# S5 branch: the lag blocks' B comes by DMA, their rows lie as (group, channel), and ScalarE places the old states

## The chip, the core and the metric

One core of a Trainium2 chip runs the kernel: TensorE (matmuls), VectorE, ScalarE and GpSimd (elementwise work), and SyncE (SP), whose queue issues every DMA of this kernel. The metric is the device time of one execution in microseconds, as the median of several runs.

## What is computed

One step of a decoder layer for a prompt of 512 tokens and 8 samples of 4 tokens (544 tokens in all, 1024 channels). The normed input is projected once; four branches (SSD, S5, mLSTM, attention into a memory) work on their columns; each is projected down, the four are merged by gates, projected out and added to the input. The change lies in the S5 branch alone:

```
lam_bar = exp(lam * dt);  b_bar = ((lam_bar - 1) / lam)[..., None] * complex(b_re, b_im)
bu = einsum('gnc,btgc->btgn', b_bar, u)          # 64 groups of 16 channels, 64 complex states each
bu[:, 0] += lam_bar * h0
h  = associative_scan(h_t = lam_bar * h_(t-1) + bu_t)
y  = einsum('gcn,btgn->btgc', c, h).real + d_skip * u
```

## The kernel before

All large products go through `unit` (line 166): a weight block of 1024x128 comes by DMA (`load`, line 80, `raw`, three buffers), is split into a high part (`whi`, ScalarE, line 177) and a low part (`wlo`, VectorE, line 64 by way of line 178), and 24 x 2 matmuls (line 188) give one `pu` of 128x544. The instructions of an engine run in the order of its queue; that order is laid down when the kernel is built, by a planner that may move an instruction ahead of others as soon as its inputs and its buffer are free in its own estimate. So the order on a queue is not always the order of the lines. Waits between engines and for buffers are put in by the same layer.

The S5 branch works in 8 rounds `f` of 128 channels, that is 8 groups of 16 channels. Time is cut into blocks of 8 steps, and a round has four parts:

- `s5_in(f)` (line 697): the input columns `pu`, copied into `uf`, turned by way of DRAM (`ud`) into `U`, with (step in block, channel) on the rows.
- `s5_mats(f)` (line 714): the matrices of the round. `bm` and `cm` are powers of lam_bar times B and C, made by VectorE and GpSimd together with temporaries `q1`, `q2`. `bbs` (line 749) is B alone, with the real parts on rows 0 to 63 and the imaginary parts on rows 64 to 127: four copies by VectorE from `bbr` and `bbi` (line 752), which `s5_setup` has made once. Eight small matmuls (line 756) of `bbs` and `cm` give `pk`, the response of one channel to another at lags 0 to 7 within a block. `pk` is copied in four pieces, by VectorE and ScalarE in turn, into `kt` (line 761), 16 rows (channel in group) by 8 groups; GpSimd makes `dk`, the skip term `d` on a diagonal, and adds it at lag 0 (lines 763, 764). `kt` goes to DRAM (`kd`, line 767) behind a stretch of zeros, and is read back (`tp`, line 769) shifted by row, so that it becomes a triangular block matrix.
- `s5_scan(f)` (line 772): `bt` times `U` gives `pv`; after a rotation by `E` (a table in `stag`, "st" in the rows, made by GpSimd in `s5_rot`, line 640, for two rounds at a time, behind rounds 0, 2 and 4) the recurrence is a real scan (lines 795, 796); rotated back it is stored in `hs` (lines 811, 812), whose first 8 columns are the samples' old states `h0`, placed by four VectorE copies (line 814). The last VectorE operations make the samples' new states `hn` from `pv` (lines 821 to 823).
- `s5_y(f)` (line 826): `tp` times `U` plus `cm` times `hs` gives `py` (lines 834, 835), copied to `yj` by ScalarE (line 836) and turned by way of DRAM (`yd`, `yt`) for `s5_out` (line 843), which applies `permid` and the GELU.

`s5_mats(f + 1)` is written behind `s5_scan(f)`. Between these parts steps of `gate_down` (line 211, `gd`) put in units of the gates and of the down projection of the attention branch: TensorE's large work in this stage. There are four PSUM banks for everything small (`bank`, line 48): `pv` takes two of them until `hn` is made, `pk`, `pbt`, `pn` and `py` take the others in turn. `bbs` and `dk` share one buffer (tag `bbs`), `hs` has one buffer, `tp` has two.

## Time and profile before

| | us |
|---|---|
| median of 3 runs | 1527.41 |
| lowest and highest | 1520.2, 1528.18 |
| the profiled execution | 1523.98 |
| its span, first to last instruction | 1522.2 |
| TensorE busy | 1446.7 |
| VectorE busy | 925.6 |
| ScalarE busy | 485.5 |
| GpSimd busy | 349.2 |

The profile names the engines PE (TensorE's matmuls), PEld (its weight loads), DVE (VectorE), ACT (ScalarE), POOL (GpSimd) and SPq (SyncE's DMA issues). All times within it are microseconds from the span's start unless marked ns. A row of instructions gives the engine, the line of the kernel (that of a helper where a helper issues it), what is written from what, and the shapes. Line 64 is every `tensor_tensor`, line 61 every copy by way of `copy`, line 67 every `scalar_tensor_tensor`. A wait is put down to the event that came last before the engine went on.

### The profile page before, as it was taken

What the parts mean: (1) busy time and instruction counts of PE and PEld (TensorE: products, weight loads), DVE (VectorE), ACT (ScalarE), POOL (GpSimd) and SP (SyncE); (2) the same over time, 40 slices, a digit from 0 to 9 for tenths busy, and PEclk for the clock granted to TensorE, in tenths of its full rate; (3) what the DMA queues carried; (4) which work ended last, traced back from release to release, by engine and by line L of the source; (5) the groups of instructions that cost most, each with busy time, mean ns of one, the idle gap of its engine ahead of it and who ended that gap; (6) DMA issues with size and microseconds to landing.
All of it is one profiled execution on the core that took longest, in us unless ns stands there. A gap on an engine that the chain in (4) does not pass through costs nothing.

```text
span 1522.2 us, 28087 instructions
## 1 busy us (share of the span) xinstructions
PE 1446.7 (95%) x11505; PEld 1364.3 (90%) x11505; DVE 925.6 (61%) x1810; ACT 485.5 (32%) x825; POOL 349.2 (23%) x527
## 2 busy tenths in 40 slices
PE   6999999789879899999999999999999999899997
PEld 6988888678768899999999989999999998789997
DVE  6355487898778768486787644354343456554543
ACT  5244333222222333243333322243332332113332
POOL 2000133766465201101232322100000011110222
PEclk9999999999789999999999999999999999999999
DMA  8577362435334333322222355222222225673341
GB/s 200 159 215 221 99 200 59 106 93 126 82 92 108 84 100 82 86 78 81 74 73 74 97 167 146 70 70 77 77 78 74 79 82 176 197 218 113 94 146 59
DMA packets 288034, 171.75 MB, mean 113 GB/s; under 512 B 36934, under 2 KB 278922, under 8 KB 287907
## 3 DMA queue, kind: packets, MB, share of 16 engines
q1 hardware_dynamic: 287906, 169.97, 40.4%
q8 instruction: 90, 1.47, 0.4%
q14 instruction: 38, 0.30, 0.1%
HBM read 145.35 MB, written 24.60 MB: 112 GB/s over the span
## 4 chain that ended last, share of the span: by engine, by line
PE 63%; DVE 10%; DMA 4%; issue 3%; POOL 2%; ACT 1%; SPq 0%; POOLq 0%; ACTq 0%; DVEq 0%
PE pu L188 48%; PE pu L1644 3%; DVE wlo L64 2%; DVE hs L64 1%; DMA raw<-in_w_out_dram 1%; DMA yd<-yj 1%; PE pacc L1557 1%; DVE bbs L752 1%; DVE cm L67 1%; PE pcu L1442 1%; DMA out_dram<-cb 1%; PE pn L1436 1%; PE py L834 1%; PE py L835 1%; DMA cb<-in_state_mlstm_c_dram 1%
## 5 line engine op out<-in xcount | busy, mean ns | idle before, releaser
L188 PE MATMUL pu<-xh,whi 128*128 128x272 f32 (+1 forms) x2000 | 432.8, 294 | 1.3 <-DVE uf L706 1.1
L188 PE MATMUL pu<-xh,wlo 128*128 128x272 f32 (+1 forms) x2000 | 428.9, 293 | 0.0
L188 PE MATMUL pu<-xl,whi 128*128 128x272 f32 (+1 forms) x2000 | 428.2, 292 | 0.6 <-DVE xl L64 0.6
L64 DVE TENSOR_TENSOR wlo<-raw,whi 128x1024 fp32r<-128x1024 f32 x181 | 251.5, 1390 | 226.3 <-ACT whi L177 221.1
L177 ACT CAST whi<-raw 128x1024 fp32r<-128x1024 f32 x181 | 198.9, 1099 | 502.6 <-PE pu L188 373.1
L188 PEld LDWEIGHTS pu<-xh,whi 128*128 128x128 f32 x2000 | 322.1, 191 | 8.3 <-issue 6.2
L188 PEld LDWEIGHTS pu<-xl,whi 128*128 128x128 f32 x2000 | 322.2, 192 | 5.6 <-issue 4.5
L188 PEld LDWEIGHTS pu<-xh,wlo 128*128 128x128 f32 x2000 | 320.2, 191 | 5.5 <-issue 5.1
L188 PE MATMUL pu<-oh,wlo 128*128 128x272 f32 x640 | 135.6, 292 | 6.0 <-DVE wlo L64 6.0
L188 PE MATMUL pu<-oh,whi 128*128 128x272 f32 x640 | 136.5, 292 | 0.0
L188 PE MATMUL pu<-ol,whi 128*128 128x272 f32 x640 | 136.4, 292 | 0.0
L188 PEld LDWEIGHTS pu<-oh,wlo 128*128 128x128 f32 x640 | 102.0, 191 | 7.7 <-DVE wlo L64 6.6
L188 PEld LDWEIGHTS pu<-ol,whi 128*128 128x128 f32 x640 | 102.7, 191 | 1.6 <-issue 1.5
L188 PEld LDWEIGHTS pu<-oh,whi 128*128 128x128 f32 x640 | 102.9, 191 | 1.0 <-issue 0.8
L64 POOL TENSOR_TENSOR merged<-merged,gt 128x544 f32<-128x544 f32 x18 | 29.1, 1616 | 142.0 <-DVE gt L67 141.9
L67 DVE SCALAR_TENSOR_TENSOR cb<-cb,dcm,pcn 128x257 f32<-128x257 f32 x64 | 28.5, 478 | 26.4 <-PE pcn L1563 26.1
L834 PE MATMUL py<-U,tp 128*128 128x72 f32 x128 | 28.3, 307 | 13.8 <-DVE hn L64 7.1
L67 DVE SCALAR_TENSOR_TENSOR cc<-cc,dcm,pcu 128x257 f32<-128x257 f32 x24 | 11.5, 478 | 44.4 <-PE pcu L1442 44.4
L188 PE MATMUL pu<-mh,whi 128*128 128x256 f32 x128 | 37.7, 294 | 0.1
L188 PE MATMUL pu<-mlo,whi 128*128 128x256 f32 x128 | 37.7, 295 | 0.0
L64 POOL TENSOR_TENSOR SS<-SS,dec 128x128 f32<-128x128 f32 x24 | 19.5, 814 | 77.6 <-DVE SS L1210 49.8
L188 PE MATMUL pu<-mh,wlo 128*128 128x256 f32 x128 | 36.2, 283 | 0.0
(641 smaller groups left out, 2297.7 us busy)
## 6 DMA issues: line engine op xcount, KB each, us to landing
raw<-in_w_in_dram SPq DMA_DIRECT2D x124, 512.0 KB
raw<-in_w_down_dram SPq DMA_DIRECT2D x32, 512.0 KB
kb<-in_cache_mem_k_dram SPq DMA_DIRECT2D x8, 1024.0 KB
raw<-in_w_mem_kv_dram SPq DMA_DIRECT2D x16, 512.0 KB
vb<-in_cache_mem_v_dram SPq DMA_DIRECT2D x16, 512.0 KB
cb<-in_state_mlstm_c_dram SPq DMA_DIRECT2D x16, 512.0 KB
out_dram<-cb SPq DMA_DIRECT2D x16, 512.0 KB
tp<-kd SPq DMA_DIRECT2D x8, 512.0 KB
```

Of the source, the lines that this page charges most:

```text
L64: eng.tensor_tensor(out, a, b, op)
L67: V.scalar_tensor_tensor(out, a, s, b, op0, op1)
L177: S.copy(hv, rv)
L188: T.matmul(ps[:, a, 0:c1 - c0], wt[:, k, :], xt[:, k, c0:c1], start=first, stop=last)
L752: V.tensor_copy(bbs[64 * ri:64 * ri + 64, :, g2, :], src[64 * g2:64 * g2 + 64, gs])
L834: T.matmul(o, tp[:, g, :], U[:, g, 0:72], start=True, stop=False)
L835: T.matmul(o, cm[:, g, 1:9, :].rearrange("p l c -> p (l c)"), hs_[:, g, 0:72], start=False, stop=True)
L1436: T.matmul(p2[:, 0:257], qh[:, dt, sl], cc[:, dt, 0:257], start=dt == 0, stop=dt == 1)
L1442: T.matmul(p3[:, 0:CE], k_[:, dt * P:(dt + 1) * P], v_, start=j == 0, stop=j == 2)
L1557: T.matmul(pacc[32 * h:32 * h + 32, 0:257], qm[:, 2 * h + dt, :], cbs_[h // 2][:, 2 * (h % 2) + dt, 0:257], start=b == 0 and dt == 0, stop ...
L1644: T.matmul(pu, wt[:, k, :], mk[:, t0:t1], start=k == 0 and j == 0, stop=k == NK - 1 and j == 2)
```

## The change

Three things, all in the S5 branch. The four VectorE copies that fill `bbs` become four DMAs from the same sources, and `bbs` gets two buffers of its own. The lag matmuls take all 32 columns of `bbs` of a pair of groups at once, so that `pk` and `kt` lie on 128 rows (4 pairs x 2 groups x 16 channels) by 2 x 128 columns; of the 2 x 2 combinations of groups only the two equal ones are used. `kt` is one ScalarE copy; the skip term is one VectorE operation on lag 0, from a column `dcol` and a constant `i16` that are made once; `dk` and GpSimd's two operations go. `kd` is written by four DMAs of 32 rows, the zeros in front of it by eight in place of two, and `tp` becomes two tiles, each read by a DMA of half the size. The old states are placed in `hs` by ScalarE, not by VectorE.

```diff
--- before.py
+++ after.py
@@ -401,11 +401,11 @@
     crs = [mtemp(512).rearrange("p (b g n) -> p b g n", b=4, g=2) for _ in range(2)]
     hrs = mtemp(512).rearrange("p (r q n) -> p r q n", r=2, q=2)
     s5b1 = mtemp(512)
-    s5b2 = mtemp(320)
+    s5b2 = mtemp(192)
     s5tmp = mtemp(384).rearrange("p (i a) -> p i a", a=32)
     ldv = mtemp(4)[0:32]
-    sdg = mtemp(16)[0:64]
-    s5_loads = [(sdg, I["s5_d"][0].rearrange("(g c) -> g c", c=16)), (ldv[:, 0:2], I["s5_log_dt"][0].rearrange("(a b) -> a b", b=2))]
+    sdg = mtemp(128)[0:8]
+    s5_loads = [(sdg, I["s5_d"][0].rearrange("(f p) -> f p", p=P)), (ldv[:, 0:2], I["s5_log_dt"][0].rearrange("(a b) -> a b", b=2))]
     for i, nm in enumerate(("re", "im")):
         s5_loads.append((arow[:, i, :], I["s5_a_" + nm][0].rearrange("(a b) n -> a (b n)", b=2)))
         s5_loads.append((bri[:, i], I["s5_b_" + nm][0].rearrange("(a b) n c -> (b n) a c", b=2)))
@@ -522,7 +522,8 @@
     h0 = pt_([P, 2, NB, 32], "h0")
     hn = pt_([P, 2, NB, 32], "hn")
     hp = pt_([P, 64], "hp")
-    d16 = pt_([16, 64], "d16")
+    dcol = pt_([P, 8], "dcol")
+    i16 = pt_([P, 16], "i16")
 
     def s5_setup():
         dtv = ldv[:, 2:4]
@@ -631,8 +632,9 @@
 
         yield
         pd = bank("pd")
-        T.transpose(pd[0:16, 0:64], sdg, ident[0:64, 0:64])
-        V.tensor_copy(d16, pd[0:16, 0:64])
+        T.transpose(pd[:, 0:8], sdg, ident[0:8, 0:8])
+        V.tensor_copy(dcol, pd[:, 0:8])
+        V.tensor_reduce(i16, ident.rearrange("p (b c) -> p c b", c=16), AX.X, ADD)
 
     hd = heads_()
     pacc = pst.tile([P, 512], F32, name="pacc4", tag="bk")
@@ -688,11 +690,12 @@
     s5d = s5c.enter_context(tc.tile_pool(name="s5d", bufs=2, space=bass.MemoryType.DRAM))
     s5r = s5c.enter_context(tc.tile_pool(name="s5r", bufs=1, side="right", reuse_waits="tile"))
 
-    kds = [s5d.tile([16, 8, 240], F32, name=f"kd{i}", tag=f"kd{i}", bufs=1) for i in range(2)]
-    kz = s5r.tile([16, 8, P], F32, name="kz", tag="kt")
+    kds = [s5d.tile([32, 4, 2, 240], F32, name=f"kd{i}", tag=f"kd{i}", bufs=1) for i in range(2)]
+    kz = s5r.tile([P, 2, P], F32, name="kz", tag="kt")
     G.memset(kz, 0.0)
     for kd in kds:
-        dma(kd[:, :, 0:112], kz[:, :, 0:112])
+        for a in range(4):
+            dma(kd[:, a, :, 0:112], kz[32 * a:32 * a + 32, :, 0:112])
 
     def s5_in(f):
         pu = unit(wcols(C_U + f * P), x2, perm=True)
@@ -746,27 +749,28 @@
             pr = slice(64 * g2, 64 * g2 + 64)
             stt(cmv[64:128, :, g2], q1[pr], -1.0, q2[pr], MUL, SUB)
 
-        bbs = s5r.tile([P, 4, 2, 16], F32, name="bbs", tag="bbs")
+        bbs = s5r.tile([P, 4, 2, 16], F32, name="bbs", tag="bbs", bufs=2)
         for ri, src in enumerate((bbr, bbi)):
             for g2 in range(2):
-                V.tensor_copy(bbs[64 * ri:64 * ri + 64, :, g2, :], src[64 * g2:64 * g2 + 64, gs])
+                dma(bbs[64 * ri:64 * ri + 64, :, g2, :], src[64 * g2:64 * g2 + 64, gs])
+
         pk = bank("pk")
         for g2 in range(2):
             for a in range(4):
-                T.matmul(pk[32 * a:32 * a + 16, g2 * P:(g2 + 1) * P], bbs[:, a, g2, :],
+                T.matmul(pk[32 * a:32 * a + 32, g2 * P:(g2 + 1) * P], bbs[:, a].rearrange("p g c -> p (g c)"),
                          cm[:, 2 * a + g2, 0:8, :].rearrange("p l c -> p (l c)"), start=True, stop=True,
                          tile_position=(0, 32 * a))
-        kt = s5r.tile([16, 8, P], F32, name="kt", tag="kt")
+        kt = s5r.tile([P, 2, P], F32, name="kt", tag="kt")
+        S.copy(kt.rearrange("p g x -> p (g x)"), pk[:, 0:256])
+        stt(kt[:, :, 0:16], bc(i16, 1, 2), dcol[:, f:f + 1], kt[:, :, 0:16], MUL, ADD)
+
+        kd = kds[f % 2]
         for a in range(4):
-            copy(S if a % 2 else V, kt[:, 2 * a:2 * a + 2, :].rearrange("p g x -> p (g x)"), pk[32 * a:32 * a + 16, 0:256])
-        dk = s5r.tile([16, 8, 16], F32, name="dk", tag="bbs")
-        tt(G, dk, bc(ident[0:16, 0:16], 1, 8), bc(d16[:, 8 * f:8 * f + 8], 2, 16), MUL)
-        tt(G, kt[:, :, 0:16], kt[:, :, 0:16], dk, ADD)
-
-        kd = kds[f % 2]
-        dma(kd[:, :, 112:240], kt)
-        tp = s5r.tile([P, 8, P], F32, name="tp", tag="tp", bufs=2)
-        dma(tp, bass.AP(tensor=kd.tensor, offset=kd.offset, ap=[[16, 8], [8 * 240, 16], [240, 8], [1, P]]))
+            dma(kd[:, a, :, 112:240], kt[32 * a:32 * a + 32])
+        tp = [s5r.tile([P, 4, P], F32, name="tp", tag=f"tp{g2}", bufs=2) for g2 in range(2)]
+        for g2 in range(2):
+            dma(tp[g2], bass.AP(tensor=kd.tensor, offset=kd.offset + g2 * (16 * 1920 + 240),
+                                         ap=[[16, 8], [1920, 16], [480, 4], [1, P]]))
         return bt, cm, tp, ev_[f // 2][:, :, f % 2]
 
     def s5_scan(f, U, bt, E):
@@ -811,7 +815,7 @@
             tt(V, hsv[0:64, :, g2, 9:73], t1[pr], t2[pr], SUB)
             tt(V, hsv[64:128, :, g2, 9:73], t3[pr], t4[pr], ADD)
             for ri in range(2):
-                V.tensor_copy(hsv[64 * ri:64 * ri + 64, :, g2, 0:8], h0[pr, ri, :, gs].rearrange("p b a -> p a b"))
+                S.copy(hsv[64 * ri:64 * ri + 64, :, g2, 0:8], h0[pr, ri, :, gs].rearrange("p b a -> p a b"))
         V.tensor_copy(hp[:, 8 * f:8 * f + 8], hs_[:, :, 72])
 
         p4 = (bc(pwr[:, 4, gs], 1, NB), bc(pwi[:, 4, gs], 1, NB))
@@ -831,7 +835,7 @@
             for g4 in range(4):
                 g = 4 * hb + g4
                 o = py[:, g4 * 72:(g4 + 1) * 72]
-                T.matmul(o, tp[:, g, :], U[:, g, 0:72], start=True, stop=False)
+                T.matmul(o, tp[g % 2][:, g // 2, :], U[:, g, 0:72], start=True, stop=False)
                 T.matmul(o, cm[:, g, 1:9, :].rearrange("p l c -> p (l c)"), hs_[:, g, 0:72], start=False, stop=True)
             S.copy(yj[:, 4 * hb:4 * hb + 4, :].rearrange("p g k -> p (g k)"), py[:, 0:288])
         yt = s5r.tile([P, 8, 72], F32, name="yt", tag="yt")
```

## Rows read from the trace of the kernel before

**Rows 1.** the page's busy line: us, share of the span, instructions of each engine

```profile
PE 1446.7 (95%) x11505; PEld 1364.3 (90%) x11505; DVE 925.6 (61%) x1810; ACT 485.5 (32%) x825; POOL 349.2 (23%) x527
```

**Rows 2.** stretches A:B: length, busy us (instructions) of each engine, clock, DMA, GB/s

```profile
250.00:530.00 280.00, 237.82 (x1918) 218.45 (x1919) 233.97 (x460) 74.36 (x127) 149.22 (x221) 0.91 0.40 95
530.00:1522.00 992.00, 975.71 (x7794) 942.49 (x7792) 547.78 (x1025) 314.77 (x521) 151.83 (x197) 0.99 0.36 103
```

**Rows 3.** TensorE's waits from 250 to 532: us in total, times, longest us

```profile
PE pk L756 <- DVE cm L67: 9.6, 7, 3.4
PE py L834 <- DVE hn L64: 7.1, 1, 7.1
PE py L834 <- DMA tp<-kd: 4.4, 1, 4.4
```

**Rows 4.** VectorE's groups by shape from 245 to 535: busy us, mean ns, idle before

```profile
L752 DVE COPY bbs<-bbr 64x64 f32<-64x64 f32 x16 | 19.5, 1218 | 0.8 <-POOL kt L64 0.5
L61 DVE COPY kt<-pk 16x256 f32<-16x256 f32 x16 | 6.6, 410 | 0.4
L814 DVE COPY hs<-h 64x32 f32<-64x32 f32 x32 | 7.9, 247 | 9.4 <-PE py L835 9.0
L64 DVE TENSOR_TENSOR hn<-hn,pvi 128x32 f32<-128x32 f32 x8 | 1.4, 180 | 0.0
```

**Rows 5.** VectorE's timeline, pairs of bbs copies: start us, us, instruction, idle before

```profile
307.92 5.41 DVE L752 COPY bbs<-bbr 64x64 f32<-64x64 f32 x2
343.91 0.39 DVE L752 COPY bbs<-bbr 64x64 f32<-64x64 f32 x2 [0.54 <-POOL kt L64]
369.75 5.20 DVE L752 COPY bbs<-bbr 64x64 f32<-64x64 f32 x2
```

**Rows 6.** the timeline around the third long pair, three engines

```profile
437.76 7.04 DVE L752 COPY bbs<-bbr 64x64 f32<-64x64 f32 x2
443.35 1.39 POOL L64 TENSOR_TENSOR st<-st,rt 128x256 f32<-128x256 f32 x2
447.58 0.70 PE L834 MATMUL py<-U,tp 128*128 128x72 f32 x2 [7.13 <-DVE hn L64]
```

**Rows 7.** TensorE's timeline after the second long pair

```profile
381.06 1.09 PE L728 MATMUL pbt<-ident,bm 128*128 128x128 f32 x8 [1.53 <-DVE bm L64]
390.62 0.63 PE L756 MATMUL pk<-cm,bbs 128*16 128x128 f32 x8 [3.39 <-DVE cm L67]
```

**Rows 8.** ScalarE from 245 to 535: a group, then two of its waits

```profile
L59 ACT COPY kt<-pk 16x256 f32<-16x256 f32 x16 | 5.8, 365 | 60.7 <-DVE kt L61 48.0 <-POOL st L64 7.4 <-issue 3.8
ACT whi L177 <- PE pu L188: 29.0, 13, 6.2
ACT yj L836 <- PE py L835: 15.8, 10, 3.1
```

**Rows 9.** SP's timeline, two issues of one round, and one of SP's waits

```profile
437.02 0.58 SPq L767 DMA_DIRECT2D kd<-kt  x1
439.38 0.63 SPq L769 DMA_DIRECT2D tp<-kd  x1
SPq L710 <- DMA ud<-uf: 32.9, 8, 4.8
```

**Rows 10.** VectorE and GpSimd during trains of GpSimd, and the group of hs

```profile
364.72 1.23 DVE L64 TENSOR_TENSOR wlo<-raw,whi 128x1024 fp32r<-128x1024 f32 x1
364.32 1.77 POOL L64 TENSOR_TENSOR st<-st,pw 128x64 f32<-128x64 f32 x2
302.64 2.62 DVE L64 TENSOR_TENSOR hs<-t,t 64x256 f32<-64x256 f32 x2
L64 DVE TENSOR_TENSOR hs<-t,t 64x256 f32<-64x256 f32 x32 | 19.6, 611 | 1.2 <-POOL t L64 0.5
```

**Rows 11.** SP's waits from 250 to 532

```profile
SPq L82 <- DVE wlo L64: 50.2, 8, 13.5
SPq L82 <- DVE s L64: 22.3, 2, 17.2
```

## The prediction

> **What bounds the kernel now.** I read the page's busy line first, then a table by stage, then who TensorE waited for in the one stage that the change touches, then the timeline around the longest of those waits. The busy line [rows 1] says TensorE: 95% of the span. A gain in work of other engines counts only where TensorE stands. The table by stage [rows 2] shows where that is: from 250 to 530 us, the S5 stage, TensorE is busy for 237.82 of 280 us, so it stands for 42.2 us, and its mean granted clock is 0.91, against 0.99 in the 992 us behind it. There VectorE is busy for 233.97 of 280 us (84%), against 55% behind (547.78 of 992). The waits of TensorE in this stage [rows 3] name VectorE nearly throughout: 9.6 us in 7 waits of the pk matmuls for cm, 7.1 us in one wait of py for hn. One wait is for a transfer (4.4 us, for tp). So inside the stage the limit is VectorE's queue, which is served in order, together with the chain of small steps that runs through it; outside the stage nothing of the change matters.
>
> **The long copies.** Of VectorE's groups in the stage [rows 4] one is out of line: 16 copies bbs<-bbr of 64x64 take 19.5 us, 1218 ns each, while a pair of the same copies takes 0.39 us where GpSimd is quiet [rows 5]. Three pairs make the difference: 5.41, 5.20 and 7.04 us. The last of them starts at 437.76 and ends at 444.80; GpSimd runs its rotation table (st, rt) without a gap until 443.35 + 1.39 = 444.74 [rows 6]. The copy waits until GpSimd's train is over. Behind it in VectorE's queue stands hn, which frees a PSUM bank, and TensorE stood 7.13 us for that before 447.58 [rows 6]. The other two have no such hole directly behind them. After the second, TensorE waited 1.53 us for bm and 3.39 us for cm [rows 7].
>
> **The change part by part.** The base is the profiled execution: 1523.98 us, of which the span is 1522.2; the median of the three times shown is 3.4 us above it, the lowest 3.8 us below.
>
> (a) bbs copies become DMAs. The three pairs are 5.41 + 5.20 + 7.04 - 3 x 0.39 = 16.5 us longer than undisturbed. What of this comes back to TensorE: the 7.1 us hole whole, of the 1.53 + 3.39 = 4.9 us half, since other work of VectorE stands in front of bm and cm too, and about 0.5 us around the first pair: 10 us. Bounds: 0, if the next VectorE instruction meets the same train of GpSimd, and 16.5. A gain above the holes is possible, since the stage's granted clock is 0.91 and may rise with fewer holes; I leave that in the range.
>
> (b) Undisturbed work leaves VectorE: 32 bbs copies at 0.19 us (half of the quiet pair), 32 hs copies at about 0.19 (a little under their mean of 0.247, which has stalls in it), 16 kt copies at 0.41 [rows 4]; 8 new scalar_tensor_tensor of 128x32 come in, which I price as the nearest 128x32 addition, 0.18 us [rows 4]. 6.1 + 6.1 + 6.6 - 1.4 = 17.4 us less in 280. It returns only where VectorE is the late one. I take a quarter, 4 us; bounds 0 and 17.4.
>
> (c) The hs copies move to ScalarE. In the stage VectorE stood 9.0 us before them, for the py matmuls to release hs [rows 4]; behind it stood the cm operations of the next group, on which pk waits. On ScalarE, the two yj copies wait for the same matmuls anyway (15.8 us in 10 waits [rows 8]), so a copy queued behind yj waits for nothing new. Work of ScalarE: 32 copies of 64x32, each between VectorE's 0.19 us and the 0.365 us of ScalarE's 16x256 copy [rows 8]; I take 0.25, so 8 us, less 8 kt copies at 0.365: 5 us more on an engine that is busy 74 of 280 us [rows 2]. I take a gain of 2 us; bounds -9 (the whole wait now stands in front of a whi cast and from there of TensorE) and +9.
>
> (d) One kt copy instead of four. Now VectorE and ScalarE alternate, and ScalarE waited 48.0 us for VectorE in that [rows 8]; two GpSimd operations, dk and the addition to kt, end the chain. Afterwards ScalarE copies once (128x256, which I price as its 16x256, 0.365 us), and VectorE adds the skip term. That shortens the way from pk to kd and frees the pk bank sooner, but TensorE waited for tp only once, 4.4 us [rows 3], so I count no gain. The added wait is VectorE's, for ScalarE's copy: behind it VectorE's whole queue stands. Bounds: nothing, if ScalarE is ready, to 6.2 us a group, the longest time that ScalarE's whi cast waited in the stage [rows 8]. I take nothing, because ScalarE idles for three quarters of the stage.
>
> (e) More transfers on SP's queue: per group four for bbs, three more for kd, one more for tp. At 0.58 to 0.63 us an issue [rows 9] that is 8 x 0.6 = 4.8 us of issuing per group, in 280 / 8 = 35 us; SP has the room. Kd takes 2.36 us from its issue to that of tp [rows 9]; with four issues in a row the last lands 3 x 0.58 = 1.7 us later, which (d)'s shorter chain should pay. Six more zero fills at the same price are 3.5 us once, at the start of the stage. A bbs transfer has 256 runs of only 64 bytes, and no row shows one alone: its bounds are kd's 2.36 us (128 runs) and the 4.8 us that SP stood at longest for ud, with 1024 runs [rows 9]; I take 2.4, nearest in count. It reads only bbr and bbi, which the setup has made before the first group, and with two buffers it can run a group ahead. I take -1 us, with 0 and -3.5 as bounds; how it could be much more is a rival.
>
> Sum: 10 + 4 + 2 + 0 - 1 = 15 us. 1523.98 - 15 = 1509 for an execution like the profiled one; with the 3.4 us to the median, **1512**.
>
> **A rule against the change.** In the quiet stretches the copies cost 0.39 us a pair, and in a train of GpSimd the whole train: that is what the rows show. The Trainium skill, page "SBUF — State Buffer", section "Who interferes with whom", says that a VectorE instruction with two SBUF inputs also contends with a GpSimd instruction that reads SBUF, and that the loser is blocked fully. By that rule, taking the copies out would only hand the stall to wlo or hs, which have two such inputs. The trace is divided: wlo at 364.72 took 1.23 us in the middle of a train, and it was GpSimd's pair beside it that stretched to 1.77 us; but a pair hs<-t,t took 2.62 us at 302.64, where the 64x256 operations of that name average 0.61 [rows 10]. By the rule the time would be the first rival's 1522, by the wlo row the forecast's 1512.
>
> **Rivals.** First, **the stall moves**: the operations that follow in VectorE's queue read two SBUF tiles, and meet the same trains. Then (a) gives nothing: 4 + 2 - 1 = 5 us, 1522. For it: hs at 302.64; against it: wlo at 364.72, which got its turn inside a train where the copies waited for the end [rows 6, 10]. Chance 0.2.
>
> Second, slower: **bbs lands too late**. SP's queue is in order, and it often stands: 50.2 us in 8 waits of the weight loads for wlo, and one of its waits for s was 17.2 us [rows 11]. In the kernel before, bbs was ready about 15 us ahead of pk (the long pair of 369.75 ends at 374.95, the next pair takes 0.4, pk runs at 390.62 [rows 5, 7]). If the four transfers are queued behind a stall like the longest, pk comes 17.2 + 4 x 0.58 + 2.4 - 15 = 6.9 us late, and the TensorE work queued behind it too. It turns the change into a loss from the third such group on (20.7 against 15). With four of the eight groups hit: 4 x 6.9 - 15 = 12.6 us lost, 1540. Against it: the second buffer and inputs that are ready early. Chance 0.12.
>
> Third, **ScalarE becomes the place to wait**: its in-order queue holds hs until py is done, and VectorE waits for kt. The 9.0 us of (c) then turn from +2 to -9: 15 - 11 = 4 us gained, 1523. Chance 0.13. Last, the order in which the instructions stand in the queues shifts, and the holes stay where they were in size: no change, 1527, chance 0.05.
>
> **How the numbers follow.** The forecast has 0.5. Its own range goes from 1497 (all of (a), half of (b), half of the 9.0 in (c): 16.5 + 8.7 + 4.5 = 30 us) to about 1519. To hold 8 in 10 the range must take in the first and third rival and the near end of the second: 1496 to 1532. The far end of the second and that of (d), 6.2 us in every group, are what I leave out. About 0.5%, 7.6 us, is what a measurement of this kernel can tell from no change. Faster by more: 0.47 of the forecast and 0.1 of the near rivals, 0.57; within: 0.30; slower: 0.13, nearly all the second rival.
>
> **What would show it.** Right: no VectorE instruction of 5 us or more in the S5 stage; TensorE's 7 us wait for hn gone; VectorE's busy time in the stage down by 25 to 35 us from 234; TensorE's idle time there down from 42 us to about 30. First rival: wlo, hs or s show up with 3 to 6 us during GpSimd's trains. Second: pk waits for a transfer of bbs. Third: waits of ScalarE for py grow, and whi is late. I am wrong if the stage is no shorter though VectorE's work has fallen: then the chain of handoffs, not the queue of VectorE, sets its pace.

## The result: a gain of 27 us, nearly twice the forecast

| | before | after |
|---|---|---|
| median, us (4 runs each) | 1525.0 | 1497.63 |
| lowest and highest | 1520.2, 1528.18 | 1491.55, 1502.62 |
| the profiled execution, its span | 1523.98, 1522.2 | 1494.56, 1492.7 |

The medians differ by 27.4 us. The ratio, taken over all runs of both kernels and therefore not exactly the quotient of the medians, is 0.9825, with an interval from 0.9804 to 0.9846: 26.7 us. The time lies inside the range, at its lower end; the forecast had 15 us. The page's busy line and the two stretches of the kernel after answer to [rows 1, 2] (a stretch: length, busy us and instructions of PE, PEld, DVE, ACT, POOL, granted clock, DMA share, GB/s). The stage ends with the last py, at 530.2 before and at 503.3 after.

```profile
PE 1438.0 (96%) x11505; PEld 1359.7 (91%) x11505; DVE 889.5 (60%) x1739; ACT 490.3 (33%) x849; POOL 340.3 (23%) x511
250.00:503.30 253.30, 232.73 (x1910) 216.18 (x1909) 196.13 (x387) 78.53 (x152) 142.34 (x205) 0.93 0.46 110
503.30:1492.00 988.70, 972.56 (x7801) 939.70 (x7800) 549.16 (x1027) 315.49 (x522) 150.50 (x197) 1.00 0.36 103
```

The stage is 26.7 us shorter. TensorE's idle time in it falls from 42.2 to 253.30 - 232.73 = 20.6 us. The other 5.1 us are TensorE's own: 237.82 us busy at a mean granted clock of 0.91 before, 232.73 at 0.93 after; busy time times clock is 216.4 us in both. The 3 us by which the rest of the span is shorter lie in unchanged work at 1.00 against 0.99. VectorE's work in the stage falls by 37.8 us.

TensorE's waits from 240 to 520 us of the kernel after (us, times, longest), to hold against [rows 3]:

```profile
PE pn L850 <- DVE bt L61: 5.6, 4, 2.3
PE py L839 <- DVE hs L64: 3.7, 1, 3.7
PE pk L760 <- issue: 3.4, 1, 3.4
PE py L838 <- DVE st L67: 3.4, 3, 1.6
PE pk L760 <- DVE cm L67: 2.1, 2, 1.8
PE py L838 <- DVE hn L64: 0.7, 1, 0.7
```

The wait for hn is down from 7.1 to 0.7 us, that for cm from 9.6 to 2.1, and none for a DMA of bbs or tp is left. The waits on which the sum rested have gone. The experiments ask which part of the change took them away.

### The profile page after: what moved, and what is told of

Read it like the earlier page. It is cut to its first block, busy times and chain, and to the rows that moved or that the text cites. A ratio compares the mean times of both kernels' runs of the same rounds, so it can differ in the third digit from the quotient of the medians.

```text
span 1492.7 us, 28127 instructions
## 1 busy us (share of the span) xinstructions
PE 1438.0 (96%) x11505; PEld 1359.7 (91%) x11505; DVE 889.5 (60%) x1739; ACT 490.3 (33%) x849; POOL 340.3 (23%) x511
## 4 chain that ended last, share of the span: by engine, by line
PE 63%; DVE 7%; DMA 5%; POOL 3%; issue 2%; ACT 1%; SPq 0%; POOLq 0%; ACTq 0%; DVEq 0%
PE pu L188 48%; PE pu L1648 3%; DMA out_dram<-cb 2%; DVE wlo L64 2%; DMA raw<-in_w_out_dram 1%; PE py L839 1%; POOL st L64 1%; PE py L838 1%; POOL q L64 1%; PE pcu L1446 1%; PE pn L1440 1%; POOL rt L64 1%; PE pst L1212 1%; PE pyi L1206 1%; PE pacc L1561 1%
```

## The experiments

The ratios below are against the kernel before as it ran beside each experiment (medians of 1522 to 1523.4 us), each with its interval; the kernel after is the one of the result above. A difference between two experiments carries both intervals. "Before" and "after" name the kernel that an edit starts from. The table reads each kernel's trace from 250 us to its last py. A trace is of one execution, which need not be the median one: it lies above the median by 7 us in k2, 6 in f1, 4 in e1 and e3, and below it by 3 in the kernel after. Idle is TensorE's, busy VectorE's. "pk held" adds up over the 8 rounds the time from the last pk matmul to the end of the last copy out of pk. "pk for cm" is the total of TensorE's wait of pk for VectorE's cm. The last column has VectorE's single instructions of over 4 us.

| kernel | median | ratio | idle | busy | pk held | pk for cm | over 4 us |
|---|---|---|---|---|---|---|---|
| before | | 1 | 42.2 | 234.0 | 72 | 9.6 | bbs 5.2, 5.0, 6.7 |
| e1_dma_only | 1517.84 | 0.9959 | 44.7 | 226.5 | 64 | 4.1 | wlo 6.0, s 6.7 |
| e2_hs_act_only | 1519.55 | 0.9977 | 39.8 | 225.4 | 71 | 12.4 | bbs 5.2, 4.5, hs 7.3 |
| e4_bbs_act | 1520.72 | 0.9979 | 41.8 | 224.3 | 68 | 11.1 | s 7.3, wlo 4.6, s 6.7 |
| m1_dma_and_hs | 1520.3 | 0.9989 | 39.3 | 217.0 | 64 | 2.4 | s 5.3, hs 7.3 |
| f1_dk_own_buffer | 1526.85 | 1.003 | 41.6 | 228.4 | 71 | 8.3 | hn 5.9 |
| g1_kt_scalar | 1524.94 | 1.0019 | 39.6 | 227.4 | 13 | 3.3 | bbs 4.8, 7.5, hs 6.4 |
| f2_skip_on_dve | 1514.06 | 0.9943 | 37.2 | 223.8 | 66 | 15.5 | none |
| l1_kt_scalar_skip_dve | 1509.49 | 0.991 | 32.3 | 218.1 | 13 | 16.3 | none |
| e3_rows_only | 1505.55 | 0.9875 | 30.8 | 213.1 | 3 | 19.0 | none |
| after | 1497.63 | 0.9825 | 20.6 | 196.1 | 3 | 2.1 | none |
| e5_after_onebuf | 1495.42 | 0.9826 | 20.3 | 196.1 | 3 | 2.0 | none |
| e6_after_bbs_dve | 1497.36 | 0.9851 | 26.1 | 205.7 | 3 | 10.0 | none |
| e7_after_hs_dve | 1496.76 | 0.9822 | 21.5 | 203.1 | 3 | 2.1 | none |
| f3_after_skip_gpsimd | 1495.93 | 0.9826 | 22.2 | 192.4 | 4 | 5.8 | none |
| k2_after_four_pieces | 1501.94 | 0.9869 | 28.9 | 201.1 | 64 | 1.8 | none |

### The three parts, one at a time

**The DMA alone** (e1; before; one buffer, shared with dk as before):

```diff
-                V.tensor_copy(bbs[64 * ri:64 * ri + 64, :, g2, :], src[64 * g2:64 * g2 + 64, gs])
+                dma(bbs[64 * ri:64 * ri + 64, :, g2, :], src[64 * g2:64 * g2 + 64, gs])
```

> The kernel before with one edit: the four bbs copies are DMAs (bbs keeps its one buffer, which it shares with dk). VectorE loses 23.6 us of bbs copies, 17.5 of them stalls. Train theory (what was paid is the long pairs behind GpSimd's trains): 15 to 20 us faster. Queue theory (every us off VectorE's queue returns at the rate of the whole change, 27 us for 38, so 0.7): 23.6 x 0.7 = 17 us faster. Chain theory (the gain comes from the shorter way from pk to kd and from the work taken off GpSimd): 0 to 5 us faster. If a bbs transfer with one buffer lands too late: slower, and pk waits for a DMA.

Measured: 1517.84 us, 0.9959 [0.9934, 0.9984], 5.5 us by the medians against the 10 of step (a). Around the place of [rows 6], the timeline of this kernel (start us, us, engine, line, instruction, idle before):

```profile
436.93 6.84 DVE L64 TENSOR_TENSOR s<-pwi,h 128x32 f32<-128x32 f32 x2
442.34 1.39 POOL L64 TENSOR_TENSOR st<-st,rt 128x256 f32<-128x256 f32 x2
445.62 0.70 PE L834 MATMUL py<-U,tp 128*128 128x72 f32 x2 [6.59 <-DVE hn L64]
```

The copies are gone and the hole is still there, 6.59 us in place of 7.13. The pair that now stands at the head of VectorE's queue reads two tiles in SBUF, s<-pwi,h; it ends at 443.77, with GpSimd's train (442.34 + 1.39 = 443.73). The group's median is 0.182 us, and one of this pair took 6.743 us. That is the first rival, at that place to the letter.

A second wait is new in this kernel. From 250 to 532 us TensorE has

```profile
PE pk L756 <- DVE hs L64: 7.1, 1, 7.1
```

which the profile puts down to hs, since an hs operation ended just then. But pk does not read hs. It reads bbs, and the trace's semaphores show the two bbs<-bbi transfers of that round, issued at 291.13 and 292.22, landing at 298.66 and 298.91; pk begins at 298.91. In m1 below the profile names the transfer for the wait at the same place. In the kernel before, this pk waited 1.7 us for VectorE's bbs. This speaks for the second rival's event here too: the DMA alone gave back part of its gain in this round. Where the time goes is seen in SP's order: in e1 and m1 the bbs<-bbi transfers of the later seven rounds are issued right behind the 512 KB read of tp and land 5.1 to 8.0 us after their issue, while the bbs<-bbr transfers ahead of tp take 1.9 to 3.0 us.

**The old states on ScalarE alone** (e2; before):

```diff
-                V.tensor_copy(hsv[64 * ri:64 * ri + 64, :, g2, 0:8], h0[pr, ri, :, gs].rearrange("p b a -> p a b"))
+                S.copy(hsv[64 * ri:64 * ri + 64, :, g2, 0:8], h0[pr, ri, :, gs].rearrange("p b a -> p a b"))
```

> The kernel before with one edit: the 32 old-state copies into hs are on ScalarE. VectorE loses 7.9 us of work, and 9.0 us of waits for py stand on ScalarE. Train theory: within 2 us of before. Queue theory: 0.7 x 7.9 = 5.5 us faster, up to 12 if the waits count too. Chain theory: no change.

Measured: 1519.55, 0.9977 [0.996, 0.9994], about 3.7 us. Two of the three long pairs of bbs stay, and in place of the third another pair meets GpSimd's train:

```profile
433.89 7.76 DVE L64 TENSOR_TENSOR hs<-t,t 64x256 f32<-64x256 f32 x2
```

**The new rows alone** (e3; after, with these three lines put back: one buffer, both kinds of copies on VectorE):

```diff
-        bbs = s5r.tile([P, 4, 2, 16], F32, name="bbs", tag="bbs", bufs=2)
+        bbs = s5r.tile([P, 4, 2, 16], F32, name="bbs", tag="bbs")
-                dma(bbs[...], src[...])
+                V.tensor_copy(bbs[...], src[...])
-                S.copy(hsv[..., 0:8], h0[...])
+                V.tensor_copy(hsv[..., 0:8], h0[...])
```

> The kernel before with the new rows alone: pk and kt on 128 rows, one ScalarE copy, skip term by one VectorE operation, GpSimd's dk and kt additions gone; bbs copies and old states stay on VectorE. VectorE loses 6.6 - 2.8 = 3.8 us, GpSimd 10.5 us. Train theory: 0 to 3 us faster, and three long bbs pairs stay. Queue theory: 0.7 x 3.8 = 3 us faster. Chain theory: 10 us or more faster.

Measured: 1505.55, 0.9875 [0.9851, 0.99], 17.7 us: two thirds of the gain from the part that step (d) had priced at nothing. First its bbs copies, then its main wait of TensorE:

```profile
L755 DVE COPY bbs<-bbr 64x64 f32<-64x64 f32 x16 | 4.6, 290 | 0.1
PE pk L760 <- DVE cm L67: 19.0, 6, 7.2
```

VectorE still makes the copies here, and they take 290 ns where [rows 4] has 1218: the long pairs are gone without a copy being moved. The largest wait left is pk for cm.

**Both without the rows** (m1; before, with the edits of the first two together):

> The kernel before with the bbs DMAs and ScalarE's old states together, without the new rows: the one combination of the three parts that is missing. Alone they gave 5.5 and 3.7 us; on top of the rows either gives 8 to 9 us and both together no more. If they add without the rows: 9 us faster than before. If without the rows pk's bank and GpSimd's late table hide them: 3 to 6 us faster, no more than the DMA alone.

Measured: 1520.3, 0.9989 [0.9973, 1.0006], no difference, where the two alone gave 5.5 and 3.7 us. VectorE has 17 us less to do in the stage, and TensorE is idle for 39.3 us. Two of VectorE's pairs, then one of TensorE's waits:

```profile
305.96 5.35 DVE L64 TENSOR_TENSOR s<-pwi,h 128x32 f32<-128x32 f32 x2
434.33 7.77 DVE L64 TENSOR_TENSOR hs<-t,t 64x256 f32<-64x256 f32 x2
PE pk L756 <- DMA bbs<-bbi: 6.6, 1, 6.6
```

The stall is handed on to s and hs, and pk waits 6.6 us once for bbs: the second rival's event, in a kernel where the buffer of bbs is shared with dk. The stage ends at 530.7 us, before it ended at 530.2. By the prediction's own sign ("I am wrong if the stage is no shorter though VectorE's work has fallen"), it is the chain of handoffs that sets the pace there, and not VectorE's queue.

**ScalarE in place of the DMA** (e4; before):

```diff
-                V.tensor_copy(bbs[...], src[...])
+                S.copy(bbs[...], src[...])
```

> The kernel before with one edit: the four bbs copies are on ScalarE in place of VectorE. This takes the same work off VectorE as the DMAs do, without a transfer. Train and queue theory: as fast as the DMA alone, 15 to 20 us faster, less at most 8 us for 8 us of new work on ScalarE. Chain theory: 0 to 5 us faster. If it equals the DMA version, the DMA is only one of two ways off VectorE's queue.

Measured: 1520.72, 0.9979 [0.9963, 0.9995]. It matters little who takes the copies: the three long stalls are there again, now in s, wlo and s. One of them:

```profile
303.06 7.45 DVE L64 TENSOR_TENSOR s<-pwi,h 128x32 f32<-128x32 f32 x2
```

### The parts undone in the kernel after

**bbs by VectorE** (e6; after; two buffers kept):

```diff
-                dma(bbs[...], src[...])
+                V.tensor_copy(bbs[...], src[...])
```

> The changed kernel with the DMA undone: VectorE copies bbs again, into two buffers of its own. If the parts add up as they did one by one (5.5 for the DMA, 3.7 for the old states, 17.7 for the rows, 27 together): 5.5 us slower than the changed kernel, about 1503. Queue theory: 6.1 us of undisturbed copies come back, 0.7 x 6.1 = 4 us slower. If the DMA only removes a collision that the rows have removed already: no slower than 2 us.

Measured: 1497.36, 0.9851 [0.9813, 0.9889]: not separable from the kernel after. Its copies, VectorE's:

```profile
L755 DVE COPY bbs<-bbr 64x64 f32<-64x64 f32 x16 | 3.6, 227 | 0.1
```

**The old states by VectorE** (e7; after):

```diff
-                S.copy(hsv[..., 0:8], h0[...])
+                V.tensor_copy(hsv[..., 0:8], h0[...])
```

> The changed kernel with the old states undone: VectorE places them again. With the new rows alone the kernel was 17.7 us faster than before, with rows and old states but VectorE's bbs copies 26 us, so the old states should be worth some 8 us on top of the rows, more than the 3.7 us alone: about 1506. If the parts only add: 3.7 us slower, about 1501. If the second bbs buffer made that difference and not the old states: no slower than 2 us.

Measured: 1496.76, 0.9822 [0.98, 0.9845]. With the rows in place the hs copies can be undone for nothing, but not both parts (e3: 8 us more). Undoing the bbs DMA (e6) costs nothing by the medians and 4 us by the ratios; its interval overlaps that of the kernel after and that of e3, so it is not settled. What the two parts have in common is relief of VectorE ahead of cm: pk's wait for cm is 19.0 us with neither, 10.0 with hs moved, 2.1 with bbs moved and 2.1 with both.

**One buffer for bbs** (e5; after):

```diff
-        bbs = s5r.tile([P, 4, 2, 16], F32, name="bbs", tag="bbs", bufs=2)
+        bbs = s5r.tile([P, 4, 2, 16], F32, name="bbs", tag="bbs")
```

> The changed kernel with one bbs buffer in place of two. The rows alone had one buffer and were 17.7 us faster than before; with the old states and two buffers 26 us, though the old states can be undone for nothing. If the second buffer makes that difference: about 8 us slower than the changed kernel, 1505. If bbs is early enough in one buffer: within 3 us.

Measured: 1495.42, 0.9826 [0.9794, 0.9859]. The second buffer is worth nothing; pk does not wait for bbs here either. In both kernels bbs has landed at least 5.8 us ahead of pk in every round.

### What in the new rows does it

Three differences in the rows are tried here: pk leaves its bank in one copy, GpSimd is out of the chain from pk to kd, and dk no longer shares a buffer with bbs. A fourth, kd in four DMAs and tp in two tiles, was not tried by itself.

**dk with a buffer of its own** (f1; before; two setup columns moved to make room):

```diff
-        dk = s5r.tile([16, 8, 16], F32, name="dk", tag="bbs")
+        dk = s5r.tile([16, 8, 16], F32, name="dk", tag="dk")
```

> The kernel before with one edit: dk has a buffer of its own, so that the bbs copies of the next group need not wait for GpSimd's addition to kt (room is made by two setup tables in scratch). New rows alone gave 17.7 us, and their trace has no long bbs pair though the copies stay on VectorE. Buffer theory (the long pairs come from the shared buffer, which puts the copies into GpSimd's train): 10 us or more faster, no bbs pair over 2 us. Queue-position theory (another operation with two SBUF inputs meets the train in their place, as s did for 6.7 us when the DMA alone was put in): 0 to 4 us faster. GpSimd theory (what counts is that GpSimd's train need no longer stand behind the kt pieces): 0 to 4 us faster.

Measured: 1526.85, 1.003 [1.0016, 1.0044], slightly slower. By itself the shared buffer was not it. But the buffer theory's event came: the long bbs pairs are gone, and one long instruction is left, of hn.

```profile
L751 DVE COPY bbs<-bbr 64x64 f32<-64x64 f32 x16 | 4.3, 271 | 0.1
```

So VectorE can lose most of its long stalls without the kernel being faster. GpSimd stands 19.3 us for ScalarE's pieces in this kernel.

**The skip term on VectorE** (f2; before; GpSimd out of the chain, the four pieces stay):

```diff
-        tt(G, dk, bc(ident[0:16, 0:16], 1, 8), bc(d16[:, 8 * f:8 * f + 8], 2, 16), MUL)
-        tt(G, kt[:, :, 0:16], kt[:, :, 0:16], dk, ADD)
+        tt(V, dk, bc(ident[0:16, 0:16], 1, 8), bc(d16[:, 8 * f:8 * f + 8], 2, 16), MUL)
+        tt(V, kt[:, :, 0:16], kt[:, :, 0:16], dk, ADD)
```

> The kernel before with one edit: dk and the addition to kt are VectorE's, no longer GpSimd's; rows, the four kt pieces and the shared buffer stay. VectorE gains 16 small operations (about 4 us), GpSimd loses 10.5 us and, above all, no longer stands in its queue until the kt pieces are done. GpSimd theory: 10 us or more faster. Buffer theory and queue theory: within 4 us, rather slower, since VectorE has more to do.

Measured: 1514.06, 0.9943 [0.9923, 0.9963]. VectorE gets 16 operations more, and the kernel is faster by 9 us; no instruction of over 4 us is left. What GpSimd loses is two operations and a place where it stood. GpSimd's waits ahead of its addition to kt in the kernel before, 250 to 532 us:

```profile
POOL kt L64 <- issue: 7.7, 2, 5.3
POOL kt L64 <- DVE hp L815: 6.1, 1, 6.1
POOL kt L64 <- ACT kt L59: 2.9, 1, 2.9
```

That is 16.7 us in which the work queued behind, its rotation table among it, does not move (for 7.7 of them the profile names no event that ended the wait). Whether this standing is what costs, g1 tells. The trains are still there: GpSimd's longest stretch of work without a gap of over 0.1 us in the stage is 17.6 us here, 20.2 before and 20.2 in the kernel after.

**All four pieces on ScalarE** (g1; before; pk's bank freed at once, GpSimd stays):

```diff
-            copy(S if a % 2 else V, kt[:, 2 * a:2 * a + 2, :].rearrange("p g x -> p (g x)"), pk[32 * a:32 * a + 16, 0:256])
+            copy(S, kt[:, 2 * a:2 * a + 2, :].rearrange("p g x -> p (g x)"), pk[32 * a:32 * a + 16, 0:256])
```

> The kernel before with one edit: all four kt pieces are ScalarE's, so that they no longer alternate with VectorE; rows, dk, GpSimd's addition and the shared buffer stay. GpSimd stood in its queue for those pieces 16.7 us in the stage of before, and where it did, its rotation table ran late, into VectorE's work. Late-table theory (what is paid is that GpSimd's table runs late because GpSimd waits for the kt pieces): GpSimd's waits before kt fall to a few us, no VectorE instruction over 4 us, 8 to 15 us faster. Work theory (what counts is VectorE's 6.6 us of kt copies): 4 us faster with the waits as they are. If the four pieces are as late on ScalarE's queue: no change.

Measured: 1524.94, 1.0019 [1.0006, 1.0033], 3 us slower, though the bank does come free. The kernel before, one round: pk, the first pn, TensorE's one wait before the next pn, then three of the last events (the last ScalarE piece, GpSimd's addition, the next pn).

```profile
391.73 0.63 PE L756 MATMUL pk<-cm,bbs 128*16 128x128 f32 x8
392.46 1.32 PE L846 MATMUL pn<-yt,permid 128*128 128x272 f32 x2
405.19 0.52 PE L188 MATMUL pu<-oh,wlo 128*128 128x272 f32 x2 [2.13 <-DVE wlo L64]
405.83 0.37 ACT L59 COPY kt<-pk 16x256 f32<-16x256 f32 x1 [3.81 <-DVE kt L61]
406.33 0.45 POOL L64 TENSOR_TENSOR kt<-kt,dk 16x128 f32<-16x128 f32 x1 [6.06 <-DVE hp L815]
406.42 1.09 PE L847 MATMUL pn<-yt,permid 128*128 128x240 f32 x2
```

The same round with all pieces on ScalarE, and VectorE's longest pair:

```profile
397.41 1.49 ACT L59 COPY kt<-pk 16x256 f32<-16x256 f32 x4 [4.25 <-PE pk L756]
399.21 1.14 PE L846 MATMUL pn<-yt,permid 128*128 128x272 f32 x2
401.83 1.02 PE L847 MATMUL pn<-yt,permid 128*128 128x240 f32 x2
365.34 7.72 DVE L752 COPY bbs<-bbr 64x64 f32<-64x64 f32 x2
```

In the kernel before the second pn (406.42) starts 0.2 us behind the last piece (405.83 + 0.37), which ends 13.8 us after pk (391.73 + 0.63). TensorE did not stand idle for that: between the two pn it works on units but for the 2.13 us wait for wlo, and its waits for the last piece add up to 0.4 us in the whole stage. If the held bank cost time in this kernel, it was through the place that pn got in the queue, which no row prices. With all pieces on ScalarE, VectorE stands in GpSimd's trains for 4.8, 7.5 and 6.4 us.

This run also answers f2's question. GpSimd's addition to kt, before and here:

```profile
L64 POOL TENSOR_TENSOR kt<-kt,dk 16x128 f32<-16x128 f32 x8 | 4.0, 500 | 16.7 <-issue 7.7 <-DVE hp L815 6.1 <-ACT kt L59 2.9
L64 POOL TENSOR_TENSOR kt<-kt,dk 16x128 f32<-16x128 f32 x8 | 4.7, 593 | 0.6 <-POOL dk L64 0.5
```

GpSimd no longer stands for the pieces (0.6 us), pk's bank is free, and still the long instructions stay and nothing is gained: the late-table theory falls in this form. What g1 keeps is GpSimd's two operations and the buffer that dk shares with bbs.

**Both** (l1; before, with the edits of f2 and g1 together):

> The kernel before with two edits that were tried one by one: all four kt pieces on ScalarE (alone: 3 us slower) and the skip term on VectorE (alone: 9.4 us faster). Rows, bbs copies, old states and the shared buffer stay. Two-lock theory (pk's bank is held by the alternating pieces, and GpSimd's table is held behind kt; taking one away leaves the other): about as much as the new rows gave, 15 to 20 us faster. If the parts only add: 6 us faster. If the rows have a merit of their own (shorter copies, smaller DMAs): 5 to 10 us faster.

Measured: 1509.49, 0.991 [0.9881, 0.9939], 13.7 us. The two edits do not merely add: their ratios multiplied give 0.9962, which lies above this interval. The two-lock theory's 15 to 20 us is not quite reached either. Against f2 alone it is 4.6 us more by the medians, with overlapping intervals. So pieces on one engine and the skip term on VectorE give 13.7 of the rows' 17.7 us together. Which locks these are is not shown: beyond g1, where the bank was free and GpSimd did not stand, this edit takes away GpSimd's two operations and its hold on the buffer of bbs. A run with the edits of f1 and g1 together would separate these; it was not made.

**Four pieces in the kernel after** (k2):

```diff
-        S.copy(kt.rearrange("p g x -> p (g x)"), pk[:, 0:256])
+        for a in range(4):
+            copy(S if a % 2 else V, kt.rearrange("p g x -> p (g x)")[:, 64 * a:64 * a + 64], pk[:, 64 * a:64 * a + 64])
```

> The changed kernel with one part undone: kt is copied in four pieces again, by VectorE and ScalarE in turn (64 columns each, on the new rows); all else stays. In the kernel before, the second pn matmul of a round started right behind the last piece, up to 10 us after pk, because pk held one of the four PSUM banks until then. Bank theory (that is what the new rows removed): most of the 18 us of the rows comes back, about 1510 to 1515. If any other part of the change covers it, as with the DMA, the old states and GpSimd's skip term, each of which could be undone for nothing: within 3 us of the changed kernel, 1494 to 1500.

Measured: 1501.94, 0.9869 [0.9839, 0.9899]; by the ratios 0.0044 or 6.7 us slower than the kernel after (4.3 by the medians), the two intervals overlapping a little. That lies between the 1510 of the bank theory and the 1500 of the other. The bank is held for 64 us again, and the wait for it appears by name among TensorE's, as it does not in the kernel after. ScalarE stands between the pieces again, too:

```profile
PE pn L852 <- ACT kt L59: 4.7, 3, 1.9
PE py L839 <- ACT kt L59: 1.9, 1, 1.9
ACT kt L59 <- DVE kt L61: 42.8, 11, 7.9
```

The two waits for the bank are 6.6 us together. But the last row is a rival: ScalarE's half of uf stands in the same queue, and TensorE's wait for uf is 4.7 us here, 6.9 in f2 and none in the kernel after (though 1.1 in the kernel before). No run separates the bank from ScalarE's queue.

The round of 380 us in the kernel after: pk, its one copy, and the second pn, which finds a free bank.

```profile
379.96 0.64 PE L760 MATMUL pk<-cm,bbs 128*32 128x128 f32 x16
380.67 0.37 ACT L764 COPY kt<-pk 128x256 f32<-128x256 f32 x1 [3.15 <-PE pk L760]
387.77 1.05 PE L851 MATMUL pn<-yt,permid 128*128 128x240 f32 x2
```

**The skip term on GpSimd** (f3; after):

```diff
-        stt(kt[:, :, 0:16], bc(i16, 1, 2), dcol[:, f:f + 1], kt[:, :, 0:16], MUL, ADD)
+        dk = s5r.tile([P, 2, 16], F32, name="dk", tag="dk")
+        tt(G, dk, bc(i16, 1, 2), bc(dcol[:, f:f + 1].to_broadcast([P, 16]), 1, 2), MUL)
+        tt(G, kt[:, :, 0:16], kt[:, :, 0:16], dk, ADD)
```

> The changed kernel with one part undone: the skip term is added by two GpSimd operations again (dk in a buffer of its own), the new rows and the one ScalarE copy stay. GpSimd theory: about 10 us slower than the changed kernel, some 1508. Piece theory (the four alternating kt copies were what cost): no slower than 3 us, about 1498. Queue theory: 2 us faster to 1 us slower.

Measured: 1495.93, 0.9826 [0.9807, 0.9846], no difference. GpSimd in the chain costs nothing here, where kt is copied within 0.4 us of pk and dk has its own buffer. Together with f2 this speaks against the work itself; with g1, also against GpSimd's standing behind the pieces as the only cause.

### Is it the trains alone?

**No rotation tables for rounds 2 to 7** (h1 from before, h2 from after):

```diff
+        if q >= 1:
+            G.memset(er, 1.0)
+            G.memset(ei, 0.0)
+            return
```

> The kernel before without GpSimd's rotation tables for rounds 2 to 7: the tables are set to constants, so these rounds rotate by nothing; everything else stays. It takes some 46 us of GpSimd's work away, and with it the trains. Late-table theory: no VectorE instruction over 4 us is left, and the kernel is 15 us or more faster than before. If the trains are not what costs: 0 to 5 us faster.

> The changed kernel without GpSimd's rotation tables for rounds 2 to 7, as in the kernel before without them. Late-table theory, strict: the trains were the difference between the two kernels, so the two without trains stand within 8 us of each other, and this one is 0 to 8 us faster than the changed kernel. If VectorE's queue is the other half: this one stays some 12 us or more ahead of the kernel before without tables.

Measured: 1511.15, 0.992 [0.9898, 0.9943] from before; 1486.33, 0.9757 [0.9739, 0.9775] from after. Without the trains the two kernels still lie 25 us apart. A theory in which the trains are the whole difference falls; they cost each kernel 10 to 12 us, also the kernel after, where no VectorE instruction is over 4 us. In the first, pk's bank is held for 78 us, in the second for 3.

**Other ways to ease the trains** (after). Buffers of their own for rt (p2), and, as a second edit of the kernel after, the tables made one step earlier (p3):

```diff
-                ts_ = [s5r.tile([P, 8 * n], F32, name="rt", tag=t) for t in ("sc1", "sc2")]
+                ts_ = [s5r.tile([P, 8 * n], F32, name="rt", tag=t) for t in ("rt1", "rt2")]
```

> A step beyond the changed kernel: the temporaries of GpSimd's rotation table (rt) get buffers of their own, where they shared those of q1 and q2. In the changed kernel VectorE stood 9.3 us in three waits of q for st, which is that sharing, and without the tables the kernel was 10 us faster. If those waits are on the path: 4 to 9 us faster than the changed kernel, 1489 to 1494. If q's other inputs are late at the same places: within 2 us.

```diff
-            if q < 1:
+            if q < 2:
-    for q in range(1):
+    for q in range(2):
         s5_rot(q)
-        if f % 2 == 0 and f // 2 + 1 in range(1, 4):
-            s5_rot(f // 2 + 1)
+        if f % 2 == 0 and f // 2 + 2 in range(2, 4):
+            s5_rot(f // 2 + 2)
```

> A step beyond the changed kernel: each of GpSimd's rotation tables is written one step earlier (the one for rounds 2 and 3 ahead of the S5 stage, where GpSimd stands idle between 240 and 260 us; the others behind rounds 0 and 2), the numbers computed are the same. Without the tables the changed kernel was 10 us faster. If a train costs by falling into the stage: a third of that, 3 us faster, 1493. If GpSimd is late for bm of round 0 instead: 2 to 5 us slower. If the order on the queues is only shuffled: within 3 us.

The kernel after has one wait that points there, VectorE's, which the kernel before does not have; VectorE still pays for the trains, now as a wait for their shared buffer:

```profile
DVE q L64 <- POOL st L64: 9.3, 3, 4.6
```

Own buffers: 1505.64, 0.9874 [0.9846, 0.9902], some 8 us slower than the kernel after, although it only takes away a wait for a buffer; why is not shown. TensorE is idle for 24.5 us in its stage, and GpSimd's work there grows from 142.3 to 153.5 us. Earlier tables: 1491.15, 0.9804 [0.9768, 0.9841]; a few us better by the median, but its interval overlaps that of the kernel after.

## Why the prediction came out right in sign and too small

**What bounds the kernel.** The stage was right: 26.7 of the 29.5 us between the two traced spans lie in it, as a fall of TensorE's idle time by 21.6 us and 5.1 us less of TensorE's own time there. The second was named as possible and left out of the sum. On what bounds the stage it was half right: it put VectorE's queue first and the chain of small steps beside it, and m1 takes 17 us of work out of the queue for nothing.

**The sign.** It came out right by luck: 12 of the 15 us stood on (a) and (c), and these two without the rows gave nothing that can be told from noise (m1). The range reached down to the measured time by terms, (a) whole and half of (b) and (c), from which the time did not come.

**(a) bbs by DMA: 10 us forecast, 5.5 measured alone, none settled in the end.** The step failed in three ways. Alone, the stall went to the next operation with two inputs (s, wlo), as the first rival said; the 5.5 us lie about midway between the 10 of the sum and the rival's 0. For this part I had let one wlo that got its turn [rows 10] weigh more than the hs pair of 2.62 us. In the change as a whole the long pairs vanish with the new rows, with the copies on VectorE (290 ns in e3, 227 in e6). They vanish with dk's own buffer too (271 ns in f1), where nothing is gained. So the right event was tied to the wrong edit, and it was not by itself what cost. Third, a transfer that I priced at 2.4 us takes 5.1 to 8.0 behind the read of tp, and pk waited for it once in e1 and m1. The Trainium skill, page "SBUF — State Buffer", section "Who interferes with whom", has it that an operation of VectorE with two inputs in SBUF contends with GpSimd's reads of SBUF: the traces of e1 and m1 agree (6.74 us in e1 for an operation whose median is 0.182).

**(b) and (c) less work of VectorE.** The amount was close: 37.8 us less busy, of which 16.5 are the long pairs, against a forecast of 25 to 35. That a quarter comes back was no property of the work. Without the rows 17 us less work (m1) returned nothing; with them, the two offloads together return 8 us, and the bbs part alone (e7) as much as both. The size of (c) was right for ScalarE. From 245 to 505 us of the kernel after, its copies, and VectorE's addition, priced at 0.18 us, which takes 0.352 in the mean (its median is 0.238, its longest 0.715):

```profile
L818 ACT COPY hs<-h 64x32 f32<-64x32 f32 x32 | 7.9, 247 | 0.3
L764 ACT COPY kt<-pk 128x256 f32<-128x256 f32 x8 | 3.0, 373 | 20.6 <-PE pk L760 20.6
L67 DVE SCALAR_TENSOR_TENSOR kt<-i,dcol,kt 128x32 f32<-128x32 f32 x8 | 2.8, 352 | 0.0
```

0.247 us against 0.25, 0.373 against 0.365. The third rival, ScalarE as the place to wait, does not show: ScalarE idles 0.3 us before the hs copies, and VectorE 0.0 before its addition.

**(d) one copy out of pk: 0 forecast, 17.7 us with the rest of the rows (e3).** This is the term that failed; two thirds of the gain came with it. The row was there: ScalarE stood 48.0 us for VectorE between the pieces [rows 8], and step (d) itself says that one copy frees the pk bank sooner. I then asked only whether TensorE waited for tp, the far end of that chain, and not who else waits along it: for the bank, in ScalarE's queue between the pieces, for the buffer that dk shares with bbs, in GpSimd's queue behind kt. The step also names GpSimd's two operations and doesn't ask what stands behind them. In its place the runs show that no single edit to this chain explains the gain: pieces on one engine gave -3 us (g1), dk's own buffer -3 (f1), the skip term on VectorE 9 (f2), and the first and the last together 13.7 (l1), more than their sum. TensorE's waits of the kernel before hardly show any of it: for the last piece they are 0.4 us there, against 3.1 in f2 and 6.6 in k2. Through which of the waits along the chain the gain comes is left open.

**(e) more issues on SP: 1 us lost forecast, no loss seen and none taken apart.** SP's issues of all eight rounds in the kernel after (count: ns shortest, median, longest; first and last start):

```profile
L755 SPq DMA_DIRECT2D bbs<-bbr x16: 597/630/1642, 251.9 to 418.2; - x16
L755 SPq DMA_DIRECT2D bbs<-bbi x16: 596/604/625, 267.2 to 424.9; - x16
L769 SPq DMA_DIRECT2D kd<-kt x32: 325/425/585, 283.1 to 479.0; - x32
```

The 0.6 us for a bbs issue was right, kd's was 0.425 and not 0.58. pk never waited for bbs, also with one buffer (e5), so the second rival falls for this kernel; its event came in e1 and m1, where the buffer is shared with dk.

**What stays open.** About 4 us between l1 (13.7) and the rows (17.7) are not taken apart; kd in four DMAs and tp in two tiles were not tried alone. How much of the 27 us is the bank, ScalarE's queue, the shared buffer or GpSimd's place can't be given as numbers. And an edit can also change the order that the planner lays down; p2, which only adds buffers, lost some 8 us. Single differences of that size between two kernels are therefore not proof of a mechanism, and the argument rests on the traces beside them.

## What to carry to other kernels

When a step frees a buffer or a bank sooner, ask who takes it next and look at the timeline there, even if no wait carries its name: where several causes end at about the same time, the table of waits shows only the last. In e1 it put 7.1 us down to hs, which the waiting instruction does not read, while the transfer that it reads had just landed. Moving an instruction that is stalled behind another engine's train handed the stall to the next one here (e1, e4, m1), and removing most of the long stalls was not yet a gain (f1). Price offloads of a busy engine after the handoffs: here 17 us of its work was worth nothing with the old handoffs in place (m1) and 8 us without them (e3 against the kernel after). And try the parts of a change in pairs too: the pair in l1 gave more than its two edits add up to.

## What was not expected of the hardware

In e1 a VectorE operation of 0.18 us was held for 6.74 us, not for one GpSimd pair (1.39 us for the one that ended the train) but to the end of a train of them without a gap. And wlo at the same line took 1.22 us and 6.00 us within one train of the same kernel (e1, at 364.26 and 369.28), so whether an instruction gets its turn inside a train isn't read from its form alone; no run here settles what decides it.

A transfer of 16 KB in runs of 64 bytes landed 1.9 to 3.0 us after its issue ahead of the 512 KB read of tp, and 5.1 to 8.0 us after its issue right behind that read (e1, m1).
